# Eight pieces of a modulation product, moved out of three SSD groups: four into the value products, four ahead of the first group's projections

## The chip, the cores and the metric

The kernel runs on one core of a Trainium2 chip. The metric is device time in microseconds (us), the median of several runs of the same program. The engines in this text: PE is TensorE (matrix products), DVE is VectorE, ACT is ScalarE, POOL is GpSimd, SP is SyncE, which here issues DMAs. Each engine takes its instructions in order; semaphores tie the engines together.

## The reference

One layer of a diffusion backbone on 512 latent tokens of width 1024, with 256 context tokens. In float32:

```python
mod = silu(c) @ w_mod + b_mod                    # 6 x 1024 numbers
sh1, sc1, gt1, sh2, sc2, gt2 = split(mod, 6)
h   = rmsnorm(x, norm1_g) * (1 + sc1) + sh1      # and the same for ctx
p   = h @ w_in       # z, xBC, dt, q, k, v and two gates, in one product
ssd = bidirectional Mamba-2 scan (4 groups x 8 heads, chunks of 128 tokens)
att = windowed attention, 16 heads on 4 key/value heads, + all context keys
x   = x + gt1 * ((g_ssd * (ssd @ w_o_ssd) + g_att * (att @ w_o_att)) @ w_out)
x   = x + gt2 * conv_ffn(rmsnorm(x, norm2_g) * (1 + sc2) + sh2)
out = rmsnorm(x, final_g)
```

What the change touches is the first line. The columns of `sh1` and `sc1` are computed at the start; the other 4096 columns (`gt1, sh2, sc2, gt2`) are needed only behind both mixers, and the kernel spreads that work over the stages before.

## The kernel before, in words

A float32 product is made of three PE products: `split` writes a weight tile as a high part `whi` (ACT, a cast from `wraw`) and a low part `wlo` (DVE, a subtraction), and `gemm` issues high x high, high x low and low x high (L197, L198, L200). `load_raw` (L145) brings each weight tile of 512 KB from SP into a ring of three buffers `wraw`; `whi` and `wlo` have two each. `run` walks a list of steps, loads one step ahead and splits ahead of the product.

Stages by the trace: modulation and norm (to 57 us); first q and k products (57 to 76); the value products, `v_step` (76 to 96), 144 products of 320 columns into five `mis` banks and one `acc` bank of PSUM, followed by the copies into `vst` (ACT L699, DVE L700) and `te` (ACT L701); attention with projections beside it (96 to 367), for which the eight banks are cut anew into `acc`, `score`, `pt` and `po`, in an order that a planner sets; the SSD (367 to 722); merges, output products and FFN (to 1230).

The SSD starts with `proj_steps(0)`, the projections of the first of four groups of heads: a product, its convolution with SiLU (ACT `ta`, DVE `ta` L1268 and L1269, ACT `tb` L1275, DVE L1276 into `BT`, `tc` or `CT`), PE transposes of the result (L1295). Then for each group `ssd_steps(g)`: states, and for each chunk of 128 tokens `chunk_in` (loads tables into the buffers `fb` with four in the ring, and makes exponentials `E` from them on ACT and DVE, L1465 to L1471), `chunk_out` (PE products `mis<-st,CT` L1480 and `mis<-E,xs` L1486) and `chunk_sum` (DVE `z`, L1506); the next group's projections stand between these.

The modulation work is `m_step(i)`, 32 pieces of 512 KB: eight groups of 512 columns (`cg`), four pieces each (`kk`). A piece is two DVE operations, each multiplying a 128 x 512 block by `silu(c)` per row and adding it into `tm` (L581 the first of a column group, L583 the others). After the fourth piece of a column group, four PE transposes (L591) put `tm` into a `mis` bank, and DVE sums it (L593) and adds the bias (L594) into `mod2`. Its place in the list before:

```python
m = msteps[3 * g : 3 * g + 3] if g < 3 else []
```

so pieces 0 to 8 stand in groups 0, 1 and 2, three each, none in group 3; 9 to 31 stand in later stages. Outside the attention's planned part, a scheduler sets the order on SP, ACT and DVE from the program's order and dependencies.

Of the kernel before, what the change touches and what calls it, by code (L numbers as in the profile page):

```python
# [18 lines left out]
P = 128  # L19
D = 1024  # L20
L = 512
# [6 lines left out]
V_BMOD = 0  # L28
# [11 lines left out]
def raw(ap):  # L40
    return ap.bitcast(F32)
# [3 lines left out]
def tile_hybrid_layer(  # L45
# [32 lines left out]
    nc = tc.nc  # L78
    V, S, G, T = nc.vector, nc.scalar, nc.gpsimd, nc.tensor
# [17 lines left out]
    def bank(name):  # L97
        pool, w, tag = banks_[name]
        return pool.tile([P, 512 * w], F32, tag=tag, name=tag)
# [8 lines left out]
    def accb():  # L108
        return bank("acc")

    def misb():
        return bank("mis")
# [3 lines left out]
    def tmp(tag):  # L116
        return tpool.tile([P, 512], F32, tag=tag, name=tag, bufs=TMP[tag])
# [21 lines left out]
        src["up", i] = wup[i], 1024  # L139
    src["dn", 0] = wdn[0, 0], 1024  # L140

    def load_raw(key):
        a, n = src[key]
        r = wpool.tile([P, 1024], F32, tag="raw", name="wraw", bufs=3)
        nc.sync.dma_start(r[:, :n], a)  # L145
        return r, n

    def split(r, n, hi, lo):
        S.copy(hi[:, :n], r[:, :n])  # L149
        V.tensor_tensor(lo[:, :n], r[:, :n], raw(hi[:, :n]), ALU.subtract)  # L150

    def split_first(r, n, hi, lo):
        V.tensor_copy(hi[:, :n], r[:, :n])
# [51 lines left out]
    ident = cpool.tile([P, P], F32, name="ident")  # L205
    vec = cpool.tile([P, NV], F32, name="vec")
# [12 lines left out]
    mod2 = cpool.tile([P, 32], F32, name="mod2")  # L219
# [84 lines left out]
    with tc.tile_pool(name="spool", bufs=1) as sp:  # L304
# [131 lines left out]
        r, W, H = {}, {}, {}  # L436
# [50 lines left out]
        rows = {}  # L487
# [47 lines left out]
        for i in range(NG):  # L535
            t = tmp("tb")
# [33 lines left out]
    def m_step(i):  # L570
        cg, kk = i // 4, i % 4

        def fn(r):
            if kk == 0:
                macc[0] = tmp("tm")
            acc = macc[0]
            for u in range(2):
                k = 2 * kk + u
                sc = csil[:, k, 0:1]
                if k == 0:  # L580
                    V.tensor_scalar_mul(acc, r[:, 0:512], sc)  # L581
                else:
                    V.scalar_tensor_tensor(acc, r[:, u * 512 : u * 512 + 512], sc, acc, ALU.mult, ALU.add)  # L583
            if kk == 3 and cg > 5:
                ps = misb()
                T.matmul(ps, ones, acc, start=True, stop=True)
                V.tensor_tensor(F["g2"][cg - 6], ps, F["g2"][cg - 6], ALU.add)
            elif kk == 3:
                ps = misb()
                for c in range(4):  # L590
                    T.transpose(ps[:, c * P : (c + 1) * P], acc[:, c * P : (c + 1) * P], ident)  # L591
                z = slice(4 * cg, 4 * cg + 4)
                V.tensor_reduce(mod2[:, z], ps.rearrange("p (c q) -> p c q", c=4), axis=AX.X, op=ALU.add)  # L593
                V.tensor_tensor(mod2[:, z], mod2[:, z], vec[:, V_BMOD + 16 + 4 * cg : V_BMOD + 20 + 4 * cg], ALU.add)  # L594

        return [("m", i)], fn

# [4 lines left out]
    a2p = a2pool.enter_context(tc.tile_pool(name="a2pool", bufs=1, reuse_waits="tile"))  # L602
# [59 lines left out]

        return [("k", t)], fn

    Q, F = {}, {}

    def q_high(r, t):
        q = [attp.tile([P, L], F32R, tag="q", name="q", bufs=7) for _ in range(2)]
# [3 lines left out]
    def q_low(r, t):  # L672

        q = Q[2 * t], Q[2 * t + 1]
        lo = tmp("tc").bitcast(F32R)
        V.tensor_tensor(lo, r, raw(q[0]), ALU.subtract)
        for o, i in ((q[1][64:128, :], q[0][64:128, :]), (q[1][0:64, :], lo[64:128, :]), (q[0][64:128, :], lo[0:64, :])):
            nc.sync.dma_start(raw(o), raw(i))

    def q_split(ps, t):  # L680
        r = rope(ps, 1.0)
        q_high(r, t)
        q_low(r, t)

    def v_step(*w):

        pos = [misb() for _ in range(5)] + [accb()]
        for k in range(KT):
            wh, wl = (z[:, (k % 3) * 320 : (k % 3 + 1) * 320] for z in w[k // 3])
            for t, po in enumerate(pos):  # L690
                hh, hl, c0 = (hlh, hll, t) if t < 4 else (hch, hcl, t - 4)
                c, o = slice(c0 * P, (c0 + 1) * P), po[:, 0:320]
                T.matmul(o, hh[:, k, c], wh, start=k == 0, stop=False)
                T.matmul(o, hh[:, k, c], wl, start=False, stop=False)
                T.matmul(o, hl[:, k, c], wh, start=False, stop=k == KT - 1)
        steps = tmp("te")
        for t, po in enumerate(pos):
            o = po[:, 0:256].rearrange("p (h d) -> p h d", h=4)
            S.copy(vst[:, t, :, 0:64], o)  # L699
            V.tensor_tensor(vst[:, t, :, 64:128], o, raw(vst[:, t, :, 0:64]), ALU.subtract)  # L700
            S.copy(steps[:, t * 64 : (t + 1) * 64], po[:, 256:320])  # L701
        F["steps"] = steps
# [86 lines left out]
    def block_atoms(n, turned):  # L789
# [27 lines left out]
        def least(i):  # L817
            h = 4 * j + i
            p = d["p"][i] = a2p.tile([P, 640], F32, tag="p", name="p", bufs=NP_)
            V.tensor_tensor_reduce(  # L820
# [61 lines left out]
        for i in range(4):  # L882
# [5 lines left out]
            needs = ["S%d.%d" % (n, i)] + (["c%d" % (n - 2)] if n > 1 else [])  # L888
            if k >= NP_:
                f, g = of(k, NP_)  # L890
                needs.append("T%d.%d.%d" % (f, (3, 4, 4, 3)[f % 4], g))
# [323 lines left out]

        return some

    NP_ = 7
    BESIDE = [("q", 2), ("q", 3), ("z", 0), ("z", 1), ("k", 1), ("q", 4), ("z", 2), ("z", 3), ("q", 5), ("z", 4)]
    BESIDE += [("q", 6), ("z", 5), ("z", 6), ("q", 7)] + [("z", i) for i in range(7, 14)] + [("oa", 0), ("oa", 1)]  # L1220
    OLD = len(BESIDE)
# [40 lines left out]
    bp = bpool.enter_context(tc.tile_pool(name="bpool", bufs=1, reuse_waits="tile"))  # L1262
# [15 lines left out]
    def flat(a):  # L1278
        return a.rearrange("p a b -> p (a b)")
# [19 lines left out]
    def proj_steps(g):  # L1299
        d = GR[g]  # L1300

        def b_fn(w):
            d["xs"] = bp.tile([P, 4, 512], F32, tag="xs", name="xs", bufs=2)
            d["xsc"] = bp.tile([P, 2, 512], F32, tag="xsc", name="xsc", bufs=1)
            d["Bkc"] = bp.tile([P, 2, P], F32, tag="Bkc", name="Bkc", bufs=2)
            d["Bk"] = bp.tile([P, 4, P], F32, tag="Bk", name="Bk", bufs=2)
            d["BT"] = bp.tile([P, L], F32, tag="BT", name="BT", bufs=2)
            pl, pc = accb(), accb()
            gemm([LAT(pl)], w)
            turn()  # L1310
            gemm([CTX(pc)], w)
            conv_silu(pl, L, 16 + g, d["BT"])
            BTc = tmp("tc")
            conv_silu(pc, LC, 16 + g, BTc)
            for t, n, k in ((d["BT"], 4, d["Bk"]), (BTc, 2, d["Bkc"])):
                TURN.append((t, n, lambda ps, n=n, k=k: S.copy(flat(k), ps[:, : n * P])))

        def c_fn(w):
            d["CT"] = bp.tile([P, L], F32, tag="CT", name="CT", bufs=2)
            pl = accb()  # L1320
            gemm([LAT(pl)], w)
            turn()
            conv_silu(pl, L, 20 + g, d["CT"])

        def x_fn(ct, w):
            i = 4 * g + ct
            pl, pc = accb(), accb()
            gemm([LAT(pl)], w)
            turn()
            gemm([CTX(pc)], w)  # L1330
            for pp, n, dst in ((pl, L, d["xs"]), (pc, LC, d["xsc"])):
                xl = tmp("tc")
                conv_silu(pp, n, i, xl)
                TURN.append(
                    (
                        xl,
                        n // P,
                        lambda ps, n=n, dst=dst: S.copy(
                            dst[:, :, ct * P : (ct + 1) * P], ps[:, :n].rearrange("p (a b) -> p a b", b=P)
                        ),  # L1340
                    )
                )

        r = [([("x", 16 + g)], b_fn), ([("x", 20 + g)], c_fn)]
        for ct in range(4):
            r.append(([("x", 4 * g + ct)], lambda w, ct=ct: x_fn(ct, w)))
        return r
# [173 lines left out]
        return r + [([], gate)]  # L1521

    msteps = [m_step(i) for i in range(32)]
    prog = proj_steps(0)
    for g in range(4):
        s = ssd_steps(g)
        f = fill[n2 + g : n2 + 1 + g]
        b = proj_steps(g + 1) if g < 3 else fill[n2 + 4 : n3]
        m = msteps[3 * g : 3 * g + 3] if g < 3 else []

        prog += s[0:1] + f + b[0:1] + s[1:2] + m[0:1] + b[1:2]
        for c in range(4):
            prog += s[3 * c + 2 : 3 * c + 3] + (s[3 * c + 4 : 3 * c + 5] if c < 3 else [])
            if g == 3 and c:
                prog += s[3 * c : 3 * c + 1]
            prog += b[2 + c : 3 + c]
            if c == 1:
                prog += b[6:]
            if g < 3 or c == 3:
                prog += s[3 * c + 3 : 3 * c + 4]  # L1540
            if c in (1, 2):
                prog += m[c : c + 1]
        prog += s[13:14]
# [649 lines left out]
```

## Time and profile before

| what | us |
|---|---|
| median of 3 runs | 1231.55 (1231.36 to 1231.83) |
| the profiled execution | 1231.67 |
| its span | 1229.8 |
| PE busy | 1217.2 |
| DVE busy | 914.8 |
| ACT busy | 687.1 |

The span runs from the first to the last recorded instruction; 1.87 us of the profiled execution lie outside it. An engine's busy time is the time in which it executed something; the rest of the span it waited. The granted PE clock was 0.998 of full speed over the run. A row of the timeline reads: start in us, duration in us, engine, line, operation, output<-inputs, shape, count, and in brackets the idle time before it and what ended that. A grouped row reads: busy us, mean ns of one | idle us before. A row of DMA issues reads: queue, count, KB each, us from issue to landing. A row of waits: engine, what it waited to do, for whom: us in total, times, longest.

### The profile page before, as it was taken

The page shows a single profiled execution, that of the slowest core. Times are in us where ns is not written, and L with a number is a line of the kernel's source. Part 1 is how long each engine was busy: PE and PEld are TensorE (multiplying, and loading weights), DVE is VectorE, ACT ScalarE, POOL GpSimd, SP SyncE. Part 2 cuts the span into 40 slices and gives each one's busy share as a digit, 9 for nine tenths or more (in the row PEclk, how much of TensorE's full clock was granted, in tenths as well). Part 3 has the DMA queues.
Part 4 walks back from the last instruction along what each step waited for, and adds up shares of the span by engine and source line. Part 5 has one row for each costly group of instructions (what it writes and reads, how often), then busy time and mean ns, then how long its engine had stood idle before and what let it go on. Part 6 is the DMA issues. An engine that isn't in the chain of part 4 may idle for free.

```text
span 1229.8 us, 17483 instructions
## 1 busy us (share of the span) xinstructions
PE 1217.2 (99%) x6337; PEld 996.6 (81%) x6337; DVE 914.8 (74%) x1489; ACT 687.1 (56%) x1302; POOL 168.0 (14%) x174
## 2 busy tenths in 40 slices
PE   9999999999999999999999999999999999999997
PEld 6798888888878877777777778888988888888886
DVE  4757888888654698697886786677688788886557
ACT  4657788787443556566586572223544444545543
POOL 0000111121100033233352530000200000000000
PEclk9999999999999999999999999999999999999999
DMA  9653678777846235345346466677144444457785
GB/s 359 250 149 91 216 203 190 213 193 218 219 143 208 92 126 147 117 131 184 122 140 201 137 204 221 230 242 236 50 164 147 145 151 152 153 169 244 245 303 200
DMA packets 108630, 224.65 MB, mean 183 GB/s; under 512 B 9600, under 2 KB 48832, under 8 KB 108544
## 3 DMA queue, kind: packets, MB, share of 16 engines
q1 hardware_dynamic: 101056, 197.32, 49.0%
q0 software_dynamic: 6912, 25.17, 8.7%
q8 instruction: 50, 0.82, 0.3%
q10 hardware_dynamic: 576, 1.05, 0.2%
q14 instruction: 36, 0.29, 0.1%
HBM read 193.29 MB, written 49.87 MB: 198 GB/s over the span
## 4 chain that ended last, share of the span: by engine, by line
PE 92%; DVE 3%; DMA 2%; ACT 2%; issue 1%; SPq 0%; POOLq 0%; ACTq 0%; DVEq 0%
PE acc L197 19%; PE acc L200 19%; PE acc L198 19%; PE acc L1919 3%; PE acc L1917 3%; PE acc L1918 3%; PE score L811 3%; PE po L860 3%; PE pt L847 2%; PE mis L1480 2%; PE mis L1385 2%; DMA wm<-wm 1%; PE acc L930 1%; PE mis L422 1%; PE acc L931 1%; PE acc L932 1%
## 5 line engine op out<-in xcount | busy, mean ns | idle before, releaser
L197 PE MATMUL acc<-hlh,whi 128*128 128x512 f32 x488 | 199.3, 408 | 0.0
L150 DVE TENSOR_TENSOR wlo<-wraw,whi 128x1024 fp32r<-128x1024 f32 (+2 forms) x119 | 143.4, 1207 | 70.1 <-ACT whi L149 60.8
L200 PE MATMUL acc<-hlh,wlo 128*128 128x512 f32 x488 | 191.4, 392 | 0.0
L149 ACT CAST whi<-wraw 128x1024 fp32r<-128x1024 f32 (+2 forms) x119 | 122.6, 1033 | 122.4 <-PE acc L198 74.5
L198 PE MATMUL acc<-hll,whi 128*128 128x512 f32 x488 | 190.8, 391 | 0.0
L197 PE MATMUL acc<-mh,whi 128*128 128x512 f32 x360 | 141.0, 392 | 0.0
L200 PE MATMUL acc<-mh,wlo 128*128 128x512 f32 x360 | 140.1, 389 | 0.0
L198 PE MATMUL acc<-ml,whi 128*128 128x512 f32 x360 | 140.0, 389 | 0.0
L200 PEld LDWEIGHTS acc<-hlh,wlo 128*128 128x128 f32 x488 | 91.6, 188 | 20.4
L198 PEld LDWEIGHTS acc<-hll,whi 128*128 128x128 f32 x488 | 91.9, 188 | 17.5 <-issue 1.7
L197 PEld LDWEIGHTS acc<-hlh,whi 128*128 128x128 f32 x488 | 91.8, 188 | 17.6 <-issue 2.2
L198 PEld LDWEIGHTS acc<-ml,whi 128*128 128x128 f32 x360 | 67.6, 188 | 14.5 <-issue 0.5
L197 PEld LDWEIGHTS acc<-mh,whi 128*128 128x128 f32 x360 | 67.6, 188 | 14.4 <-issue 0.5
L200 PEld LDWEIGHTS acc<-mh,wlo 128*128 128x128 f32 x360 | 67.6, 188 | 14.0
L820 DVE CUSTOM_DVE_ANT_0 p<-score,winm,nsink 128x512 f32<-128x512 f32 (+1 forms) x64 | 51.8, 810 | 15.0 <-PE score L811 13.6
L1268 DVE SCALAR_TENSOR_TENSOR ta<-acc,half,ta 128x511 f32<-128x511 f32 (+1 forms) x66 | 43.8, 663 | 25.8 <-ACT ta L1267 25.8
L1267 ACT ACTIVATE ta<-acc,half 128x512 f32<-128x512 f32 (+1 forms) x66 | 46.8, 709 | 27.1 <-PE acc L200 25.9
L1275 ACT ACTIVATE tb<-ta 128x512 f32<-128x512 f32 (+1 forms) x44 | 23.5, 534 | 65.0 <-DVE ta L1269 59.0
L827 ACT ACTIVATE p<-p,mneg 128x512 f32<-128x512 f32 (+1 forms) x64 | 49.7, 777 | 15.3 <-DVE mneg L820 14.7
L1387 POOL TENSOR_TENSOR st<-st,eT 128x512 f32<-128x512 f32 x24 | 33.5, 1396 | 170.6 <-ACT st L1405 162.3
L197 PE MATMUL acc<-hch,whi 128*128 128x256 f32 x176 | 54.4, 309 | 0.0
L855 DVE TENSOR_TENSOR ptl<-pt,pth 128x512 fp32r<-128x512 f32 x72 | 47.5, 686 | 8.6 <-ACT pth L851 7.8
(512 smaller groups left out, 2972.7 us busy)
## 6 DMA issues: line engine op xcount, KB each, us to landing
wraw<-wup SPq DMA_DIRECT2D x44, 512.0 KB, 3.6
wt_d<-wdn POOLq DMA_DIRECT2D x36, 512.0 KB, 7.5
fb<-cs_d SPq DMA_DIRECT2D x32, 512.0 KB, 6.6
wraw<-wm SPq DMA_DIRECT2D x32, 512.0 KB, 4.3
wraw<-wx SPq DMA_DIRECT2D x24, 512.0 KB, 3.5
wraw<-wt_d SPq DMA_DIRECT2D x20, 512.0 KB, 4.3
sp_d<-te SPq DMA_DIRECT2D x33, 256.0 KB, 2.5
wm<-wm SPq DMA_DIRECT2D x16, 512.0 KB, 7.7
```

The source lines that it names most:

```text
L149: S.copy(hi[:, :n], r[:, :n])
L150: V.tensor_tensor(lo[:, :n], r[:, :n], raw(hi[:, :n]), ALU.subtract)
L197: T.matmul(ps, wh, xh[:, k0 + k, :], start=a, stop=False)
L198: T.matmul(ps, wh, xl[:, k0 + k, :], start=False, stop=False)
L200: T.matmul(ps, wl, xh[:, k0 + k, :], start=False, stop=b)
L811: T.matmul(ps[:, o : o + len(z) * P], Q[h][:, b * P : (b + 1) * P], k[:, j, z[0] * P : (z[-1] + 1) * P], start=v == 0 and o % 512 in (0, P ...
L820: V.tensor_tensor_reduce(p[:, :w], d["ps"][i][:, o0 : o0 + w], m, op0=ALU.add, op1=ALU.min, scale=1.0, scalar=nsink[:, h : h + 1], accum_o ...
L827: S.activation(p, p, AF.Exp, bias=d["mneg"][:, i : i + 1], scale=-1.0, accum_out=d["den"][:, i : i + 1])
L855: V.tensor_tensor(d["ptl"][x], d["pt"][x], raw(d["pth"][x]), ALU.subtract)
L860: T.matmul(d["po"], vst[:, cols[x], j, :], d[y][x], start=x == 0 and y == "pth", stop=x == c - 1 and y == "ptl")
L1267: S.activation(o[:, :n], ps[:, :n], AF.Identity, scale=hcol(base_w, stride + i), bias=hcol(base_b, i))
L1268: V.scalar_tensor_tensor(o[:, 1:n], ps[:, 0 : n - 1], hcol(base_w, i), o[:, 1:n], ALU.mult, ALU.add)
```

## The change

Pieces 0 to 3 (column group 0) are brought in `v_step` by eight DMAs of 128 x 512 into buffers that the attention will use later (`p`, six; `pth`, two). Their eight DVE operations are ordered behind the last `wlo` before the value products; the transposes and the sum follow the last value product and come ahead of the copies into `vst` in the program. Pieces 4 to 7 (column group 1) are brought by four DMAs into the ring `fb` before the first group's projections; their eight DVE operations stand there too, and their transposes and sum follow the third step of those projections. Piece 8 stays in group 0; groups 1 and 2 have none.

```diff
-            elif kk == 3:
-                ps = misb()
-                for c in range(4):
-                    T.transpose(ps[:, c * P : (c + 1) * P], acc[:, c * P : (c + 1) * P], ident)
...
+            elif kk == 3 and F.get("later"):
+                F["close"] = lambda: close(acc)
             elif kk == 3:
+                close(acc)
+        def close(acc):      # the lines taken out above: transposes, sum, bias
...
     def v_step(*w):
-        pos = [misb() for _ in range(5)] + [accb()]
+        pieces = []
+        for i in range(4):
+            if i < 3:
+                r = [a2p.tile([P, 640], F32, tag="p", name="p", bufs=NP_)[:, :L] for _ in range(2)]
+            else:
+                r = [raw(a2p.tile([P, L], F32R, tag="pth", name="pth", bufs=2)) for _ in range(2)]
+            for u in range(2):
+                nc.sync.dma_start(r[u], wm2[0, i, :, u * L : u * L + L])
+            pieces.append(r)
+        behind = F["low"].ins            # the last wlo
+        v_products(w)
+        with tc.issue_after(behind):
+            for i in range(4):
+                m_step(i)[1](pieces[i])
+        v_rows()
...
     msteps = [m_step(i) for i in range(32)]
+    mfirst = {0: msteps[8:9], 1: [], 2: [], 3: []}
+    pieces = []
+    for i in range(4):
+        f = bp.tile([P, 8, P], F32, tag="fb", name="fb", bufs=4)
+        nc.sync.dma_start(flat(f), wm2[1, i])
+        pieces.append(flat(f))
+    F["later"] = True
+    for i in range(4):
+        m_step(4 + i)[1](pieces[i])
+    F["later"] = False
     prog = proj_steps(0)
+    prog.insert(3, ([], lambda: F["close"]()))
...
-        m = msteps[3 * g : 3 * g + 3] if g < 3 else []
+        m = mfirst[g]
```

Line numbers grow by about 30 in the later parts. PE at the end of the value products, with what each instruction waits for (semaphores, by engine); first before, then changed:

```order
L694 MATMUL acc<-wlo,hch 128x320
L695 MATMUL acc<-whi,hcl 128x320
L811 MATMUL score<-khi,q 128x256 [waits DMAHW7_49,DMAHW4_49,Activation_49]
L811 MATMUL score<-klo,q 128x256 [waits DMAHW6_49]
L811 MATMUL score<-khi,q 128x256
L811 MATMUL score<-klo,q 128x256
L197 MATMUL acc<-hlh,whi 128x512
```

```order
L722 MATMUL acc<-wlo,hch 128x320
L723 MATMUL acc<-whi,hcl 128x320
L599 MATMUL mis<-ident,tm 128x128 [waits Activation_49]
L599 MATMUL mis<-ident,tm 128x128 x3
L841 MATMUL score<-khi,q 128x256 [waits DMAHW5_49,DMAHW1_49,DVE_49]
L841 MATMUL score<-klo,q 128x256 [waits DMAHW3_49]
L841 MATMUL score<-khi,q 128x256
L841 MATMUL score<-klo,q 128x256
L199 MATMUL acc<-hlh,whi 128x512
```

Four transposes of `tm` now stand between the last value product and the first score. The score waited for ACT's last copy out of the first value bank; now the transposes wait for that copy, and the score waits for DVE's sum out of the same bank. DVE at the same place, before and changed:

```order
L150 TENSOR_TENSOR wlo<-wraw,whi 128x640
L944 TENSOR_TENSOR wlo<-wraw,whi 128x1024
L700 TENSOR_TENSOR vst<-mis,vst 128x4x64 x5
L700 TENSOR_TENSOR vst<-acc,vst 128x4x64
L820 ISA p,mneg<-score,winm,nsink 128x512
```

```order
L152 TENSOR_TENSOR wlo<-wraw,whi 128x640
L584 TENSOR_SCALAR tm<-p,csil 128x512
L586 SCALAR_TENSOR_TENSOR tm<-p,csil,tm 128x512 x5
L586 SCALAR_TENSOR_TENSOR tm<-pth,csil,tm 128x512 x2
L974 TENSOR_TENSOR wlo<-wraw,whi 128x1024
L730 TENSOR_TENSOR vst<-mis,vst 128x4x64 x5
L730 TENSOR_TENSOR vst<-acc,vst 128x4x64
L601 TENSOR_REDUCE mod_89<-mis 128x4
L602 TENSOR_TENSOR mod_89<-mod_89,vec 128x4
L850 ISA p,mneg<-score,winm,nsink 128x512
```

The eight products stand between the two `wlo`; the sum stands behind all six subtractions into `vst`, ahead of the first softmax operation. DVE at the first group's projections, before and changed:

```order
L150 TENSOR_TENSOR wlo<-wraw,whi 128x1024 x2
L1268 SCALAR_TENSOR_TENSOR ta<-acc,half,ta 128x511
L1269 SCALAR_TENSOR_TENSOR ta<-acc,half,ta 128x511
L1276 SCALAR_TENSOR_TENSOR BT<-tb,ta 128x512
L1268 SCALAR_TENSOR_TENSOR ta<-acc,half,ta 128x255
L1269 SCALAR_TENSOR_TENSOR ta<-acc,half,ta 128x255
L150 TENSOR_TENSOR wlo<-wraw,whi 128x1024
L1276 SCALAR_TENSOR_TENSOR tc<-tb,ta 128x256
```

```order
L586 SCALAR_TENSOR_TENSOR tm<-fb,csil,tm 128x512 x2
L1297 SCALAR_TENSOR_TENSOR ta<-acc,half,ta 128x511
L586 SCALAR_TENSOR_TENSOR tm<-fb,csil,tm 128x512
L1298 SCALAR_TENSOR_TENSOR ta<-acc,half,ta 128x511
L586 SCALAR_TENSOR_TENSOR tm<-fb,csil,tm 128x512 x2
L1305 SCALAR_TENSOR_TENSOR BT<-tb,ta 128x512
L586 SCALAR_TENSOR_TENSOR tm<-fb,csil,tm 128x512
L1297 SCALAR_TENSOR_TENSOR ta<-acc,half,ta 128x255
L586 SCALAR_TENSOR_TENSOR tm<-fb,csil,tm 128x512
L1298 SCALAR_TENSOR_TENSOR ta<-acc,half,ta 128x255
L152 TENSOR_TENSOR wlo<-wraw,whi 128x1024
L1305 SCALAR_TENSOR_TENSOR tc<-tb,ta 128x256
```

Seven of the eight products now stand between the operations of one convolution (the first stands ahead of the rows shown), all ahead of the `wlo` and the `tc` that PE takes next. PE's transposes of that `tc` moved behind one matmul of the next product. SP at that place, before and changed:

```order
L145 DMA wraw<-wx 128x1024
L972 DMA ao_d<-te 128x512
L145 DMA wraw<-wx 128x1024
L1433 DMA z<-zs_d 128x512 x2
L972 DMA ao_d<-te 128x512
L145 DMA wraw<-wx 128x1024
L1433 DMA z<-zs_d 128x512 x2
L1445 DMA fb<-cs_d 128x8x128 x4
```

```order
L147 DMA wraw<-wx 128x1024
L1002 DMA ao_d<-te 128x512
L147 DMA wraw<-wx 128x1024
L1557 DMA fb<-wm 128x1024
L1002 DMA ao_d<-te 128x512
L1557 DMA fb<-wm 128x1024 x3
L147 DMA wraw<-wx 128x1024
L1462 DMA z<-zs_d 128x512 x4
L1474 DMA fb<-cs_d 128x8x128 x2
```

One load of a piece stands ahead of the store `ao_d<-te`, three behind it and ahead of the third `wraw<-wx`; the loads `z` and the first tables `fb<-cs_d` come after. In group 1, two `tm` stood in DVE's row between `xw` and the first `E` (L1469); that place is now:

```order
L1305 SCALAR_TENSOR_TENSOR CT<-tb,ta 128x512
L1485 SCALAR_TENSOR_TENSOR coef<-TT,cbd,bcs 128x8
L1402 TENSOR_TENSOR xw<-xs,TD 128x512
L1498 COPY_PREDICATED E<-sel,eb 128x512
L1500 TENSOR_TENSOR E<-E,mis 128x512
```

The first `E` follows `xw` directly.

More of the change, by code (lines that the diff above doesn't have):

```diff
@@ L140, in tile_hybrid_layer @@
     src["dn", 0] = wdn[0, 0], 1024
+    F = {}
     def load_raw(key):
@@ L149, in split @@
         S.copy(hi[:, :n], r[:, :n])
-        V.tensor_tensor(lo[:, :n], r[:, :n], raw(hi[:, :n]), ALU.subtract)
+        F["low"] = V.tensor_tensor(lo[:, :n], r[:, :n], raw(hi[:, :n]), ALU.subtract)
     def split_first(r, n, hi, lo):
@@ L576, in fn @@
             acc = macc[0]
+            rows = r if isinstance(r, list) else [r[:, u * 512 : u * 512 + 512] for u in range(2)]
             for u in range(2):
@@ L580, in fn @@
                 if k == 0:
-                    V.tensor_scalar_mul(acc, r[:, 0:512], sc)
+                    V.tensor_scalar_mul(acc, rows[0], sc)
                 else:
-                    V.scalar_tensor_tensor(acc, r[:, u * 512 : u * 512 + 512], sc, acc, ALU.mult, ALU.add)
+                    V.scalar_tensor_tensor(acc, rows[u], sc, acc, ALU.mult, ALU.add)
             if kk == 3 and cg > 5:
@@ L587, in fn @@
                 V.tensor_tensor(F["g2"][cg - 6], ps, F["g2"][cg - 6], ALU.add)
+            elif kk == 3 and F.get("later"):
+                F["close"] = lambda: close(acc)
             elif kk == 3:
-                ps = misb()
-                for c in range(4):
-                    T.transpose(ps[:, c * P : (c + 1) * P], acc[:, c * P : (c + 1) * P], ident)
-                z = slice(4 * cg, 4 * cg + 4)
-                V.tensor_reduce(mod2[:, z], ps.rearrange("p (c q) -> p c q", c=4), axis=AX.X, op=ALU.add)
-                V.tensor_tensor(mod2[:, z], mod2[:, z], vec[:, V_BMOD + 16 + 4 * cg : V_BMOD + 20 + 4 * cg], ALU.add)
+                close(acc)
+        def close(acc):
+            ps = misb()
+            for c in range(4):
+                T.transpose(ps[:, c * P : (c + 1) * P], acc[:, c * P : (c + 1) * P], ident)
+            z = slice(4 * cg, 4 * cg + 4)
+            V.tensor_reduce(mod2[:, z], ps.rearrange("p (c q) -> p c q", c=4), axis=AX.X, op=ALU.add)
+            V.tensor_tensor(mod2[:, z], mod2[:, z], vec[:, V_BMOD + 16 + 4 * cg : V_BMOD + 20 + 4 * cg], ALU.add)
         return [("m", i)], fn
@@ L663, in k_step @@
         return [("k", t)], fn
-    Q, F = {}, {}
+    Q = {}
     def q_high(r, t):
@@ L683, in q_split, with v_products @@
         q_low(r, t)
+    NP_ = 7
     def v_step(*w):
-        pos = [misb() for _ in range(5)] + [accb()]
+        pieces = []
[13 more added lines that the diff above has]
+        v_rows()
+    def v_products(w):
+        pos = F["pos"] = [misb() for _ in range(5)] + [accb()]
         for k in range(KT):
@@ L695, in v_step, with v_rows @@
                 T.matmul(o, hl[:, k, c], wh, start=False, stop=k == KT - 1)
+    def v_rows():
         steps = tmp("te")
-        for t, po in enumerate(pos):
+        for t, po in enumerate(F.pop("pos")):
             o = po[:, 0:256].rearrange("p (h d) -> p h d", h=4)
@@ L1216, in weight_sums @@
         return some
-    NP_ = 7
     BESIDE = [("q", 2), ("q", 3), ("z", 0), ("z", 1), ("k", 1), ("q", 4), ("z", 2), ("z", 3), ("q", 5), ("z", 4)]
```

## The prediction

> **What bounds the kernel now.** I read the page's busy shares first, then its chain that ended last, then TensorE's waits in the SSD stage (300 to 730 us), where most of the moved work stands today.
>
> ```profile
> PE 1217.2 (99%) x6337; PEld 996.6 (81%) x6337; DVE 914.8 (74%) x1489; ACT 687.1 (56%) x1302; POOL 168.0 (14%) x174
> PE 92%; DVE 3%; DMA 2%; ACT 2%; issue 1%; SPq 0%; POOLq 0%; ACTq 0%; DVEq 0%
> ```
>
> TensorE (PE) is busy 99% of the span and carries 92% of the chain; VectorE (DVE), which this change relieves in one place and loads in another, carries 3%. So only what makes PE wait counts. The four head groups, one per stretch, then the modulation products (`tm`) on DVE in the same stretches:
>
> ```profile
> 420.00:500.00 80.00, 79.75 (x444) 61.30 (x443) 67.07 (x104) 48.17 (x114) 24.44 (x18) 1.00 0.41 128
> 500.00:580.00 80.00, 79.02 (x441) 60.60 (x440) 65.41 (x103) 50.03 (x117) 29.93 (x21) 1.00 0.47 143
> 580.00:660.00 80.00, 79.48 (x446) 61.64 (x445) 65.43 (x104) 50.60 (x118) 31.52 (x22) 1.00 0.47 145
> 660.00:722.00 62.00, 62.00 (x297) 44.23 (x296) 43.10 (x67) 40.48 (x98) 28.42 (x21) 1.00 0.49 154
> 420.00:500.00 80.00, 6.99 (x6) 1.00 0.41 128
> ...
> 660.00:722.00 62.00, 0.00 (x0) 1.00 0.49 154
> PE mis L1486 <- DVE E L1471: 0.9, 1, 0.9
> PE mis L1385 <- DVE z L1506: 0.5, 1, 0.5
> ```
>
> In the first rows the columns after the stretch's length are PE, PE's weight loads, DVE, ACT, POOL; the short rows are DVE's `tm` time alone, for the first and the last stretch. The three groups with pieces leave PE idle 0.25 + 0.98 + 0.52 = 1.75 us; the fourth, without pieces, leaves 0.00. The waits name 1.4 us of it, a row at 485 us below the rest. That is the whole prize in these groups, however much DVE work leaves them.
>
> **Part 1, what leaves the groups.** Eight pieces go, one (piece 8) stays: 16 DVE products, and with each closed column group four PE transposes, a reduction and an addition.
>
> ```profile
> L583 DVE SCALAR_TENSOR_TENSOR tm<-wraw,csil,tm 128x512 f32<-128x512 f32 x15 | 15.8, 1056 | 1.4 <-DMA wraw<-wm 1.2
> L581 DVE TENSOR_SCALAR tm<-wraw,csil 128x512 f32<-128x512 f32 x3 | 1.4, 478 | 1.6 <-DMA wraw<-wm 1.6
> L593 DVE TENSOR_REDUCE mod<-mis 128x4 f32<-128x512 f32 x2 | 1.4, 675 | 0.0
> 539.23 0.66 PE L1486 MATMUL mis<-E,xs 128*64 128x128 f32 x8
> 540.78 0.66 PE L1486 MATMUL mis<-E,xs 128*64 128x128 f32 x8 [0.90 <-DVE E L1471]
> 533.41 2.33 DVE L583 SCALAR_TENSOR_TENSOR tm<-wraw,csil,tm 128x512 f32<-128x512 f32 x2
> 540.04 0.69 DVE L1471 TENSOR_TENSOR E<-E,mis 128x512 f32<-128x512 f32 x1
> 633.96 1.09 PE L1486 MATMUL mis<-E,xs 128*64 128x128 f32 x16
> 635.57 1.12 PE L1385 MATMUL mis<-xw,Bk 128*128 128x512 f32 x2 [0.52 <-DVE z L1506]
> 633.42 1.10 DVE L1276 SCALAR_TENSOR_TENSOR tc<-tb,ta 128x512 f32<-128x512 f32 x1 [0.76 <-ACT tb L1275]
> 479.41 1.67 DVE L583 SCALAR_TENSOR_TENSOR tm<-wraw,csil,tm 128x512 f32<-128x512 f32 x1 [0.59 <-DMA wraw<-wm]
> 485.27 1.13 PE L1480 MATMUL mis<-st,CT 128*128 128x512 f32 x2 [0.25 <-ACT xs L1338]
> ```
>
> About 14 x 1.056 + 2 x 0.478 = 15.7 us of DVE time leave, off PE's path but for three places. At 540 us, 2.33 us of `tm` stand in DVE's queue ahead of the chain of exponents (`E`) that PE waits for. By starts, that wait is worth more than its 0.90: eight `mis<-E,xs` took 540.78 - 539.23 = 1.55, while sixteen took 1.09 at 633.96, so eight are near 0.5 and 1.05 is lost. All of it goes, since E ends 0.9 after PE wants it and 2.3 is taken out ahead. At 485 us a `tm` of 1.67 that itself waited 0.59 for its weights stands ahead of the exponents that ACT waits for before its copy `xs`; start to start I put 0.4 on it, and it goes. At 635.6 no `tm` product stands ahead in DVE's queue: `tc` there waited for ACT, and the reduction comes after `z`. I leave that 0.5 where it is. Next to be late is ACT: it already releases `tc`, with 0.76. **Gain 1.5 us; ends 0 (another wait follows each) and 2.1 (all three by starts, the one on `z` being 635.57 - 633.96 less about 1.0).** The eight PE transposes and the reductions only move; weight loads on SP also only move.
>
> **Part 2, four pieces in the value products (76 to 96 us).** Eight DMAs of 256 KB and eight DVE products enter; the transposes follow the last value product, and the scores take over the bank that they fill.
>
> ```profile
> 91.87 1.23 DVE L944 TENSOR_TENSOR wlo<-wraw,whi 128x1024 fp32r<-128x1024 f32 x1 [7.46 <-ACT whi L941]
> 94.23 2.18 DVE L700 TENSOR_TENSOR vst<-mis,vst 128x256 fp32r<-128x256 f32 x5 [1.13 <-ACT vst L699]
> 96.43 0.42 DVE L700 TENSOR_TENSOR vst<-acc,vst 128x256 fp32r<-128x256 f32 x1
> 96.77 0.74 DVE L820 CUSTOM_DVE_ANT_0 p<-score,winm,nsink 128x512 f32<-128x512 f32 x1
> 95.83 0.28 PE L811 MATMUL score<-khi,q 128*128 128x256 f32 x1
> 84.31 0.58 SPq L145 DMA_DIRECT2D wraw<-wq  x1
> wraw<-wq SPq DMA_DIRECT2D x2, 512.0 KB, 4.1
> 90.00:94.00 4.00, 4.00 (x29) 4.00 (x29) 1.23 (x1) 1.23 (x2) 0.00 (x0) 1.00 0.00 0
> ```
>
> The products cost nothing: 0.48 + 7 x 0.75 = 5.7 us fit in DVE's idle 7.46 ahead of 91.87, from 84.4 on. The last two of the eight DMAs are issued on SP where `wraw<-wq` goes out now, 84.3; with its 4.1 us they land by about 88.6 and DVE is free by 90.2, ahead of that `wlo`. SP's two `wq` loads behind them move some 1.2 us back, and the bus is empty (0.00) from 90 to 94 to take that up. The close does cost. PE used to start the first score at 95.83. Now the transposes run first (four at 0.11 from start to start, 0.44, no addition, since they leave the groups), to 96.27; the first score then waits for the reduction, which stands behind `vst<-acc` on DVE and so begins where `p<-score` began, 96.77, and takes 0.68 by its own row: 97.45, and 0.05 to PE. PE's queue behind that score holds the first of the projections, so nothing fills the gap. **Loss 97.5 - 96.3 = 1.2 us; ends 0.8 and 1.5**, by DVE and ACT reaching `vst<-acc` up to 0.4 earlier or 0.3 later.
>
> **Part 3, four pieces before the first group (364 to 382 us).** Four loads of 512 KB go out on SP around the store `ao_d<-te`, ahead of the third `wraw<-wx`, and the eight products interleave with the convolution on DVE.
>
> ```profile
> 373.79 0.75 DVE L1268 SCALAR_TENSOR_TENSOR ta<-acc,half,ta 128x511 f32<-128x511 f32 x1 [4.22 <-ACT ta L1267]
> 378.73 0.42 DVE L1276 SCALAR_TENSOR_TENSOR tc<-tb,ta 128x256 f32<-128x256 f32 x1
> 381.56 0.38 PE L1295 MATMUL mis<-ident,tc 128*128 128x128 f32 x2
> 382.24 0.40 PE L200 MATMUL acc<-hlh,wlo 128*128 128x512 f32 x1
> 368.82 0.32 SPq L972 DMA_DIRECT2D ao_d<-te  x1
> wraw<-wx SPq DMA_DIRECT2D x3, 512.0 KB, 4.4
> fb<-cs_d SPq DMA_DIRECT2D x2, 512.0 KB, 8.0
> ```
>
> The first piece can leave before 368 us and its two products fall into DVE's idle 4.22. The other three leave after that store, from about 369.2; at 4.0 to 4.4 us the second lands near 373.2, and the rest while DVE is at work. From there DVE holds six `tm` (4.0 us at the 0.67 from one start to the next), two long `ta` (1.6), BT (0.6), two short `ta` (0.9), `wlo` (1.1) and `tc` (0.4): 8.7, to 381.9. `tc` ended at 379.15 before, so the slack is nearly eaten: PE transposed `tc` at 381.56, but one matmul has been put ahead of it, so it is wanted at about 381.8, and `wlo`, done near 381.5, at 382.2. **Loss 0.15 us; ends 0 and 1.0**, for a second piece 0.2 early or 0.9 late. The deferred close adds only its transposes, 0.44, which left the groups. The four loads of `fb<-cs_d` wait for buffers that the products free, and land some 40 us before the stage that reads them.
>
> [...] If all three landed with the last, at about 375.6, the sum would be 1233.7, with the second piece 2.4 late; that is the milder form of rival A.
>
> **Sum.** The profiled execution took 1231.67 us (span 1229.8), 0.12 above the median of 1231.55. 1231.67 - 1.5 + 1.2 + 0.15 = **1231.5 us**. A measurement of this kernel tells 0.2%, 2.5 us, from no change, hardly less.
>
> **Rivals.** *A, slower: the pieces land late before the first group.* DVE works in order, so a `tm` that waits for its weights holds `ta`, `wlo` and `tc` behind it, and PE stops at 381.8. The price is the lateness less the slack. At 8.0 us, as `fb<-cs_d` had, the second piece lands at 377.2, 4.0 late; PE then stands 4.0, and the time is 1231.5 - 0.15 + 4.0 = 1235.3. It decides (over 1234.0) from 2.7 late. For it: four loads leave almost together. Against: 4.4 us was the median for `wraw<-wx` on the same queue in these 13 us. *B, no gain in the groups:* ACT, which already releases DVE there, takes the place of each wait: 1231.5 + 1.5 = 1233.0. For it: the waits at 485 and at 635 both run through ACT. Against: at 540 the chain has 2.3 us of `tm` directly ahead. *C, the close doesn't hold the scores:* DVE gets through the reduction before PE asks, and Part 2 is free: 1231.5 - 1.2 = 1230.3, with all 2.1 gained 1229.7. Against: the reduction is ordered behind `vst<-acc`. *D, DVE bounds the groups after all:* the 15.7 us come off in full, 1231.5 + 1.5 - 15.7 = 1217.3; against it stands the 1.75 us idle of PE.
>
> ```profile
> 1000.00:1100.00 100.00, 100.00 (x441) 82.45 (x440) 83.03 (x125) 47.62 (x70) 0.00 (x0) 1.00 0.47 153
> 646.33 1.88 PE L1480 MATMUL mis<-st,CT 128*128 128x512 f32 x4
> ```
>
> D has one more reading. The first four windows hold 227.77 us of weight loads in 302, 75.4%, where pure products hold 82.45%; that looks like 26 us of hidden waiting. But undisturbed SSD products start 1.88 / 4 = 0.47 apart at most, against 100 / 441 = 0.23, with one load each either way, so slower products explain the low share. [...]
>
> **How the numbers follow.** Forecast 0.52; A beyond 1234.0, 0.11; B and the milder A up to 1234.0, 0.21; C 0.11; D, or part of it below 1229.0, 0.05. The range leaves out A's 0.11, D's 0.05 and little else: from C with all the gain, 1229.7, to B with Part 3 at its end, 1233.85, and 0.2 more on either side for the scatter of the runs (1231.36 to 1231.83): 1229.5 to 1234.0. Faster by over 0.2%: D, 0.05, and a tail of C, 0.01. Slower: A, 0.11. Within: 0.83.
>
> **What would show it.** Right: in the changed profile the first score starts near 97.5 with about 1.2 us idle, released by DVE's reduction; the `tm` on `p` and `pth` lie between 84 and 91; `tc` ends near 381.9 and PE is idle by 0.2 or less there; the wait of PE on `E` in group 1 is gone and the one on `z` stays. Wrong: a wait of PE on DVE between 375 and 390 of over 1 us; a second large wait in the attention stage, where everything starts 1.65 later; or new waits on ACT in groups 0 to 2.

## The result, and the profile after

The changed kernel takes 1229.54 us (19 runs, 1228.99 to 1230.80) where the kernel before took 1231.75 in the same series: ratio 0.9982, 95% interval 0.9975 to 0.9989. In a later series it was 1229.45, ratio 0.9979 (0.9970 to 0.9988). So 2.2 us are gained; the forecast was 1231.5 us, next to no gain on the 1231.55 known then. The profiled execution took 1229.21 us, its span is 1227.4.

The page's busy shares and chain, then PE's whole list of waits, of the changed kernel:

```profile
PE 1216.9 (99%) x6337; PEld 997.3 (81%) x6337; DVE 912.9 (74%) x1489; ACT 686.4 (56%) x1302; POOL 166.1 (14%) x174
PE 96%; DMA 2%; DVE 1%; ACT 0%; issue 0%; SPq 0%; POOLq 0%; DVEq 0%; ACTq 0%
PE acc L457 <- POOL still L350: 1.1, 1, 1.1
PE score L841 <- DVE mod L601: 1.1, 1, 1.1
PE acc L243 <- DVE nsink L487: 0.3, 1, 0.3
PE acc L376 <- DMA wm<-wm: 0.2, 1, 0.2
```

DVE's busy time is nearly the same, 912.9 us after 914.8: the work has moved. Its share of the chain fell from 3% to 1%. All three waits of the SSD groups are gone, and one new wait stands at the first score. The groups' stretches (columns as in the prediction):

```profile
420.00:500.00 80.00, 80.00 (x450) 62.21 (x449) 63.66 (x99) 48.78 (x116) 23.66 (x18) 1.00 0.34 104
500.00:580.00 80.00, 80.00 (x447) 62.19 (x446) 61.98 (x98) 50.93 (x119) 29.30 (x21) 1.00 0.43 133
580.00:660.00 80.00, 80.00 (x447) 62.21 (x446) 61.49 (x97) 51.26 (x121) 31.01 (x22) 1.00 0.45 136
660.00:722.00 62.00, 62.00 (x294) 44.22 (x294) 43.66 (x66) 41.02 (x97) 30.15 (x22) 1.00 0.49 153
```

PE has no idle time left there, and in the first three stretches 450, 447 and 447 matmul records stand where there were 444, 441 and 446. The end of the value products, PE and then DVE:

```profile
95.39 0.31 PE L723 MATMUL acc<-whi,hcl 128*128 128x320 f32 x1
95.54 0.60 PE L599 MATMUL mis<-ident,tm 128*128 128x128 f32 x4
97.22 0.39 PE L841 MATMUL score<-khi,q 128*128 128x256 f32 x1 [1.08 <-DVE mod L601]
96.14 0.42 DVE L730 TENSOR_TENSOR vst<-acc,vst 128x256 fp32r<-128x256 f32 x1
96.48 0.68 DVE L601 TENSOR_REDUCE mod<-mis 128x4 f32<-128x512 f32 x1
```

PE stops for the sum, which stands behind the last subtraction into `vst`. The first group's projections, DVE and then PE:

```profile
374.26 0.75 DVE L586 SCALAR_TENSOR_TENSOR tm<-fb,csil,tm 128x512 f32<-128x512 f32 x1 [2.27 <-DMA fb<-wm]
381.35 1.22 DVE L152 TENSOR_TENSOR wlo<-wraw,whi 128x1024 fp32r<-128x1024 f32 x1
382.49 0.41 DVE L1305 SCALAR_TENSOR_TENSOR tc<-tb,ta 128x256 f32<-128x256 f32 x1
383.01 0.39 PE L1324 MATMUL mis<-ident,tc 128*128 128x128 f32 x2
383.47 0.39 PE L202 MATMUL acc<-hlh,wlo 128*128 128x512 f32 x1
```

DVE starts on the second piece as it lands, at 374.26; everything there stands 1.2 us later than before, and `tc` and `wlo` are done just ahead of PE.

To see where the 2.4 us of the two spans went, I matched PE's instructions of the two traces in their order and took the difference of their starts (after less before; each step is a change of that difference):

| place (time in before) | difference behind it | step | what it is |
|---|---|---|---|
| start, to 57 | -0.24 | -0.24 | the first weights: PE waited 1.4 for them, now 0.2 |
| first score, 95.83 | +1.39 | +1.63 | transposes 0.44, wait 1.19 |
| attention, to 355 | +1.22 | -0.17 | +0.11 right behind the first score, whose successor starts 0.22 after it and not 0.11; -0.28 at a wait on `de` that is gone |
| projections, 382 | +1.14 | -0.08 | nothing |
| 390 | +1.60 | +0.46 | transposes of column group 1 |
| 485 to 487 | +0.84 | -0.76 | group 0: ACT `xs`, then `E` |
| 518 | +0.34 | -0.50 | transposes that left |
| 540 to 570 | -1.42 | -1.76 | group 1: 1.10 on `E`, 0.66 in three smaller steps |
| 632 | -1.86 | -0.44 | transposes that left |
| 635 to 637 | -2.57 | -0.71 | group 2: the wait on `z` |
| the end, 1222 | -2.43 | +0.14 | nothing of the change |

The transposes cancel (+0.90, -0.94). What is left is +1.30 at the scores (1.19 and 0.11) and -3.23 in the groups.

### The profile page after: what moved, and what is told of

Its sections match the earlier page's. It is cut to its first block, busy times and chain, and to the rows that moved or that the text cites. A ratio compares the mean times of both kernels' runs of the same rounds, so it can differ in the third digit from the quotient of the medians.

```text
span 1227.4 us, 17505 instructions
## 1 busy us (share of the span) xinstructions
PE 1216.9 (99%) x6337; PEld 997.3 (81%) x6337; DVE 912.9 (74%) x1489; ACT 686.4 (56%) x1302; POOL 166.1 (14%) x174
## 3 DMA queue, kind: packets, MB, share of 16 engines
q10 hardware_dynamic: 576, 1.05, 0.2%
## 4 chain that ended last, share of the span: by engine, by line
PE 96%; DMA 2%; DVE 1%; ACT 0%; issue 0%; SPq 0%; POOLq 0%; DVEq 0%; ACTq 0%
PE acc L199 20%; PE acc L202 20%; PE acc L200 20%; PE acc L1957 3%; PE acc L1959 3%; PE acc L1958 3%; PE score L841 3%; PE po L890 3%; PE pt L877 2%; PE mis L1509 2%; PE mis L1414 2%; PE mis L1515 1%; DMA wm<-wm 1%; PE acc L960 1%; PE acc L962 1%; PE acc L961 1%
```

## The experiments

Each was timed against the kernel before in the same series (1231.79 to 1231.88 us there).

**The halves.** Pieces 0 to 3 in the value products, the others in the groups:

```diff
-    mfirst = {0: msteps[8:9], 1: [], 2: [], 3: []}
+    mfirst = {0: [], 1: [nop] + msteps[4:6], 2: msteps[6:9], 3: []}
     # nop is a step that does nothing; no pieces are taken ahead of proj_steps(0)
```

> The changed kernel with only its first half: pieces 0 to 3 in the value products; pieces 4 and 5 stay in group 1, 6 to 8 in group 2, group 0 has none. Theory (the gain sits where pieces leave a group, and the close costs the scores 1.2 us): +1.2 at the scores, -0.8 for group 0, between 0 and -1.3 in group 1, nothing in group 2, so 1231.0 to 1232.2 against 1231.75 for before. Rival (the gain is a lucky order of the attention or of the scheduler, not the pieces): near the changed kernel, 1229.5, or near before plus 1.2, 1233, wherever the pieces stand.

It took 1234.57 us, ratio 1.0019 (1.0010 to 1.0027): slower than before by 2.7, outside what I expected. Its trace agrees with the theory up to 1100 us, where it stands 1.0 ahead of the kernel before (+1.67 at the scores, -0.74 in group 0, -1.40 at 540 in group 1). Then comes a wait in the FFN that neither the kernel before nor the changed kernel has. PE's longest wait and its row:

```profile
PE acc L1948 <- DVE tc L1842: 2.5, 1, 2.5
1115.04 0.47 PE L1948 MATMUL acc<-ww,fyh 128*128 128x512 f32 x1 [2.53 <-DVE tc L1842]
```

This is the first product of the down part. For it the eight banks are cut anew into `acc`, and its first bank is bank 0. In this kernel the last up product, which DVE still reads at L1842, had come to stand in bank 0 of PSUM too; in the kernel before it stands in bank 1, in the changed kernel in 2. Its place in the ring of five `mis` banks follows from how the banks went round since the ring was made, and a close taken out ahead moves it.

The other half, pieces 4 to 7 ahead of the projections and 0 to 3 left in groups 0 and 1, 8 in group 2:

```diff
-    mfirst = {0: msteps[8:9], 1: [], 2: [], 3: []}
+    mfirst = {0: msteps[0:3], 1: msteps[3:4], 2: [nop, nop, msteps[8]], 3: []}
     # and v_step without pieces
```

> The changed kernel with only its second half: pieces 4 to 7 ahead of the first group's projections; 0 to 2 stay in group 0, 3 in group 1, 8 at the end of group 2. Theory: no wait at the scores, 0 to +0.2 in the projections, group 0 as before, group 1 and group 2 gain 1.3 to 2.4: 1229.4 to 1230.6. Rival (order by luck): no gain, 1231.7.

It took 1231.22 us, ratio 0.9994 (0.9985 to 1.0003): no gain that is clear of the scatter. As expected, there is no wait at the scores and none in the projections (the step there is -0.04), group 1 gains 1.7, and in group 2 the wait on `z` is gone (-0.72). But 1.7 is lost again in group 2, by starts, in two waits on `E` (1.12 and 0.62; the list of waits shows 1.3 of it). The larger comes behind these rows of DVE; what makes the smaller, at 648, was not traced:

```profile
611.69 1.28 DVE L584 TENSOR_SCALAR tm<-wraw,csil 128x512 f32<-128x512 f32 x1
613.01 1.67 DVE L586 SCALAR_TENSOR_TENSOR tm<-wraw,csil,tm 128x512 f32<-128x512 f32 x1
619.37 0.69 DVE L1487 TENSOR_TENSOR E<-E,mis 128x512 f32<-128x512 f32 x1
PE mis L1502 <- DVE E L1487: 1.3, 2, 0.9
```

Piece 8 has moved: before, its two products ran at 643.6, since `tm` has one buffer and column group 1 held it until its transposes at 631.7. With that group closed long before, they run as soon as their weights are there, ahead of `E`, and take 2.95 us where the pair at 643.6 took 1.22.

**The bank.** Values only, with one more bank taken from the ring at the end of the SSD (a write of one column), and the changed kernel with the same line:

```diff
     run(prog)
+    for _ in range(1):
+        V.memset(misb()[:, 0:1], 0.0)
     bpool.close()
```

> Values only again, with one bank of the mis ring taken (a write of one column, 128 x 1) and never used at the end of the SSD, so that the last product of the FFN's up part stands in bank 3 and not in bank 0, which the first down product takes over. Theory: the 2.5 us wait of PE on DVE at 1113 us was that shared bank; it goes, and 1231.87 + 1.2 - 2.2 = 1230.9 is left. Rival (the wait is the pieces' late DVE work): 1234.5 as before.

> The changed kernel with one bank of the mis ring taken in the same way, which puts its last up product into bank 0 (2 without this). Theory: the same wait of 2.5 us appears at the first down product, and nothing else changes: 1229.54 + 2.7 = 1232.2, so the changed kernel's gain would be lost to a bank number 700 us later. Rival: the wait belonged to the other kernel alone, 1229.5.

The line puts the last up product into bank 3 in the first and into bank 0 in the second. The first took 1230.94 us, ratio 0.9992 (0.9983 to 1.0001): the wait is gone, and the theory's number holds. The second took 1233.11 us, ratio 1.0010 (1.0001 to 1.0018): the wait has come, and with it the changed kernel is slower than the kernel before. It came out 0.9 above what I expected; the last section shows where that comes from. The rows show the wait, a PE row further on, and the granted clock (the column after POOL) in 1112 to 1120 us:

```profile
1113.39 0.47 PE L1959 MATMUL acc<-ww,fyh 128*128 128x512 f32 x1 [2.53 <-DVE tc L1853]
1115.41 0.63 PE L1960 MATMUL acc<-ww,fyl 128*128 128x512 f32 x1
1112.00:1120.00 8.00, 6.61 (x22) 5.31 (x23) 7.96 (x13) 4.98 (x8) 0.00 (x0) 0.79 0.83 286
```

Up to that point the two changed kernels' traces differ by 0.2 us at most. So the bank explains the wait in both directions. Without it the median of "values only" lies 0.9 us below the kernel before, in an interval that still holds no difference.

**The close.** The transposes of pieces 0 to 3 go into a free `acc` bank, ahead of the last eighth of the value products; the products are ordered ahead of `v_products` in the program, still behind the last `wlo`:

```diff
...                                     # close takes the bank as an argument
-        behind = F["low"].ins
-        v_products(w)
-        with tc.issue_after(behind):
+        F["later"] = True
+        with tc.issue_after(F["low"].ins):
+            for i in range(4):
+                m_step(i)[1](pieces[i])
+        F["later"] = False
         v_products(w)
...
         for k in range(KT):
+            if k == KT - 1:
+                F["close"](accb())
```

> The changed kernel with the close of pieces 0 to 3 moved: the four transposes go into a free acc bank ahead of the last eighth of the value products, and the sum stands ahead of the subtractions into vst. Theory: the products are done 2.9 us before the transposes, the first score finds its bank without DVE's sum, the wait of 1.1 goes: 1229.54 - 1.2 = 1228.3. Rival: the scores then wait for something else that ends as late (ACT's copies, or vst set back by the sum's 0.8 us), and the time stays within 0.4 of 1229.5.

It took 1228.40 us, ratio 0.9971 (0.9961 to 0.9981). PE's rows and DVE's sum, from the profile of the repeat below:

```profile
93.21 0.60 PE L599 MATMUL acc<-ident,tm 128*128 128x128 f32 x4
96.14 0.31 PE L726 MATMUL acc<-whi,hcl 128*128 128x320 f32 x1
96.29 0.28 PE L844 MATMUL score<-khi,q 128*128 128x256 f32 x1
93.84 0.69 DVE L601 TENSOR_REDUCE mod<-acc 128x4 f32<-128x512 f32 x1 [0.63 <-PE acc L599]
```

The first score follows the last value product at once. The sum falls into time in which DVE was idle: its first `vst` starts at 94.69, 1.45 us ahead of PE's last value product, as in the changed kernel (93.94 against 95.39). Since 1.1 us is little beside the scatter of the runs, both ran again in one series:

> The changed kernel itself, beside the early close on one chip: 1229.5.

> The early close again, beside the changed kernel. Theory: 1.2 below it, 1228.3. Rival (the difference was between chips): within 0.4 of it.

They took 1229.45 us (ratio 0.9979, 0.9970 to 0.9988) and 1228.40 (0.9971, 0.9960 to 0.9982). That is 1.05 us apart, where the first runs, in two series, lay 1.14 apart. Between these two traces the start of the first score steps by -1.59, of which 0.4 are the transposes that now stand earlier. This is the fastest of the kernels that do all the work. The intervals of the two ratios overlap; that it is faster rests on the repeat, on the medians and on the wait that is gone.

**What the pieces cost in the groups.** Without pieces 0 to 7; and with their loads alone:

```diff
-        m = msteps[3 * g : 3 * g + 3] if g < 3 else []
+        m = msteps[8:9] if g == 0 else []                       # no pieces
...
+    V.memset(mod2, 0.0)                                         # in both
+    msteps[:8] = [(k, lambda r: None) for k, _ in msteps[:8]]   # loads only
```

> The kernel before without pieces 0 to 7, which are left out altogether (their columns of mod2 are set to zero); piece 8 stays in group 0. Theory: everything the eight pieces cost before goes: waits of 3.2 us and eight transposes, 0.9: 1231.75 - 4.1 = 1227.6. So the changed kernel pays 1.2 for the close, 0.9 for transposes and nothing for the sixteen DVE products. Rival (DVE work hides more than waits show): under 1226.

> The kernel before with pieces 0 to 7 loaded in their places into wraw, but their sixteen DVE products, the transposes and the sums left out (their columns of mod2 are zero). Theory (the DVE products were what held PE): as without the pieces, 1227.4 to 1227.8. Rival (the weight loads in the ring of three, or the DMA traffic, held the next weights): most of the 3.2 us of waits stay, 1230 to 1231.

Without pieces it took 1227.44 us, ratio 0.9965 (0.9952 to 0.9977), the theory's number. PE stands 4.4 ahead at the end, by the same steps in the groups as in the changed kernel, which lies 2.1 above it: the close and eight transposes. With the loads only it took 1229.43 us, ratio 0.9980 (0.9971 to 0.9989), below the rival's range and far above the theory's. Groups 0 and 1 gain in full (-0.74 and -1.76 without the transposes), and 1.8 is lost again at 618 and 634. The first of these two places:

```profile
609.35 1.28 DVE L581 TENSOR_SCALAR tm<-wraw,csil 128x512 f32<-128x512 f32 x1
610.67 1.67 DVE L583 SCALAR_TENSOR_TENSOR tm<-wraw,csil,tm 128x512 f32<-128x512 f32 x1
618.12 0.66 PE L1486 MATMUL mis<-E,xs 128*64 128x128 f32 x8 [0.90 <-DVE E L1471]
```

It is piece 8 again, which this kernel left in group 2. With piece 8 taken in group 0:

```diff
-        m = msteps[3 * g : 3 * g + 3] if g < 3 else []
+        m = msteps[3 * g : min(3 * g + 3, 8)] if g < 3 else []
...
-        prog += s[0:1] + f + b[0:1] + s[1:2] + m[0:1] + b[1:2]
+        prog += s[0:1] + f + b[0:1] + s[1:2] + m[0:1] + (msteps[8:9] if g == 0 else []) + b[1:2]
```

> Loads only, as the last one of that kind, but with piece 8 taken in group 0 instead of group 2, where its two DVE products had moved up to 609 us and ahead of E. Theory (loads cost PE nothing; the 2.0 us between the two kernels were piece 8's place): as the kernel without pieces, 1227.4 to 1227.8, no wait of PE at 617 and 632. Rival (the loads of pieces 6 and 7 hold something in group 2): 1229.0 to 1229.5 again.

It took 1227.83 us, ratio 0.9968 (0.9956 to 0.9979): as without pieces, by the same steps of PE, and with no wait in group 2. So the loads cost PE nothing that these runs show; the DVE work of the pieces did, products and sums together. And this one piece in a bad place costs 1.8 us by starts (1.6 by the two medians), about half of the 3.2 that the eight others cost before.

**The slack of the projections.** Two more products there:

```diff
         m_step(4 + i)[1](pieces[i])
+    for u in range(2):
+        V.scalar_tensor_tensor(macc[0], pieces[3][:, u * L : u * L + L], csil[:, u, 0:1], macc[0], ALU.mult, ALU.add)
```

> The changed kernel with two more products of the same form in the first group's projections (the last piece added in twice more, which changes column group 1 of mod2), 1.3 us of DVE ahead of wlo and tc. Theory (the slack of that place is eaten to about 0.2 us): PE stops there for 1.0 to 1.3 us, and the time is 1230.5 to 1230.8. Rival (slack is left): 1229.5 to 1229.8, no wait of PE between 375 and 390.

It took 1229.75 us, ratio 0.9983 (0.9974 to 0.9992): the rival's number, though PE does lose 0.74 at that place. The order had changed with it: `tc` went ahead of the last product, and PE had two products on context rows and the deferred transposes to put into the gap,

```profile
383.94 0.28 PE L200 MATMUL acc<-hcl,whi 128*128 128x256 f32 x1
384.06 0.60 PE L599 MATMUL mis<-ident,tm 128*128 128x128 f32 x4
384.66 0.50 PE L202 MATMUL acc<-hlh,wlo 128*128 128x512 f32 x1
```

so a part of the work that stood later in the changed kernel (the transposes at 391.36) was done while it waited. This run therefore doesn't measure the slack itself. How late the loads may come (rival A) wasn't tried.

## Why the prediction was right or wrong

The time lies 0.04 us inside the lower edge of the range, 1229.5, and in the later series, at 1229.45, 0.05 outside it. That it lies inside is luck: I had set that edge for a close that costs nothing and all of the gain that I held possible (rival C), but the close cost what I forecast, and the groups gave more. The sum was 2.0 us too high, 1.7 of it in one term. By its steps:

*The close at the scores* (1.2): it cost 1.19 up to the first score, released by DVE's sum, and 1.30 up to the second; the kernel without this wait is 1.05 to 1.14 faster by the medians. Right in mechanism and size.

*The projections* (0.15): they cost nothing (the step is -0.08). The second piece was there 1.06 later than the 373.2 forecast, on a stage that stood 1.2 later, and `tc` ended at 382.90, against 381.9 + 1.2. Right; rival A didn't come. The 8.0 us of `fb<-cs_d` that I set against it were no case of four loads leaving together: SP issued those four from 370.99 to 378.17, behind loads of `z`. Here three pieces were issued from 370.43 to 371.81, and they took 3.7, 4.9 and 5.8 us, so they came one behind the other and not all with the last.

*The products in the value stage* (nothing): right; they ran from 84.04 to 90.04 in one row.

*The gain in the groups* (1.5, ends 0 and 2.1): this is the step that failed. It measured 3.23, beyond its upper end; the kernels without the eight pieces' DVE work confirm it. The parts: 485 us, 0.76 for my 0.4; 540 us, 1.76 for my 1.05; 635 us, 0.71 for my 0. Two errors are in it. First, I took each listed wait and the one place it stood at. PE's first start behind `E` gained 1.10, near the 1.05 that I worked out, but three smaller steps behind it (0.30, 0.23, 0.13) are in no list of waits, because PE is drawn as busy there. The second of them, in the kernel before, stands in four products that undisturbed take 1.88:

```profile
565.80 2.11 PE L1480 MATMUL mis<-st,CT 128*128 128x512 f32 x4
```

The 0.23 are inside the 2.11. So the idle 1.75 us, which I called the whole prize, were no upper bound. Second, I kept the wait on `z` because no `tm` stood directly ahead of it and ACT released the row before. But DVE works through a backlog there. In the changed kernel all the work there stands earlier, and one operation stands behind `z` and not ahead; DVE before, then changed:

```profile
634.45 0.47 DVE L1268 SCALAR_TENSOR_TENSOR ta<-acc,half,ta 128x255 f32<-128x255 f32 x1
634.84 0.67 DVE L1506 TENSOR_TENSOR z<-mis,z 128x512 f32<-128x512 f32 x1
630.92 1.26 DVE L1305 SCALAR_TENSOR_TENSOR tc<-tb,ta 128x512 f32<-128x512 f32 x1 [0.76 <-ACT tb L1304]
632.11 0.68 DVE L1535 TENSOR_TENSOR z<-mis,z 128x512 f32<-128x512 f32 x1
633.84 0.47 DVE L1297 SCALAR_TENSOR_TENSOR ta<-acc,half,ta 128x255 f32<-128x255 f32 x1
```

Against before, `z` is 2.73 earlier and PE there 2.44. Most of it is the backlog: `tc`, ahead of `z`, already starts 2.50 earlier (633.42 before); it still waits 0.76 for ACT, but that wait moved along with the rest. Likewise at 540: in "values only" both products of the 2.33 us row still stand directly ahead of `E`, yet the wait is gone. What had left DVE's queue there are two other products and the sum and addition of column group 0; before, then "values only":

```profile
522.94 0.68 DVE L593 TENSOR_REDUCE mod<-mis 128x4 f32<-128x512 f32 x1
525.34 0.47 DVE L581 TENSOR_SCALAR tm<-wraw,csil 128x512 f32<-128x512 f32 x1
525.86 0.75 DVE L583 SCALAR_TENSOR_TENSOR tm<-wraw,csil,tm 128x512 f32<-128x512 f32 x1
532.35 2.33 DVE L586 SCALAR_TENSOR_TENSOR tm<-wraw,csil,tm 128x512 f32<-128x512 f32 x2
```

From 520 to that row DVE gains 1.86 on the kernel before, 0.8 behind it at first and 1.06 ahead at the end (532.35 for 533.41). The row that I named was not the cause by itself.

*Rivals.* B (ACT takes the place of each wait) didn't come: no wait of PE is left there. C didn't come in this kernel; the early close shows what it is worth. D didn't come: 15.7 us of DVE left the groups and PE got 3.2 back; without the eight pieces at all it gets 4.4, with their transposes. The low share of weight loads, which looked like 26 us of hidden waiting, is 230.84 of 302 us now, 76.4% after 75.4%, with every wait gone: slower products, as the sum had it.

What stays open: the 0.24 at the start and the 0.28 at the wait on `de` in attention, 0.5 together. The first differs between the profiles of all these kernels (-0.31 to +0.29 against before, at 57 us). The second stands in every profile of a kernel with pieces in the value products (eight) and in none without (four, where the wait on `de` stays); what links it to them I didn't test.

## What to carry to other kernels

Where an in-order engine feeds the bottleneck just in time, size the relief by the backlog that leads up to a late operation, not by the row ahead of it (here 3.23 us came for the 1.5 read off the rows ahead), and compare starts of the bottleneck's instructions rather than its idle time. A small work unit that closes a product should find a bank and a place in the queue ahead of the evacuations that the next stage waits for (here 1.1 us). After any change that alters how often a ring of banks is used, look at the next place where the banks are cut anew: there a shift of one or two banks was worth more (2.6 us and over) than the whole change.

## What the runs showed that I had not expected

Behind the same wait of 2.53 us the granted clock was 1.00 in the profile of "values only" (1.00 in 1112 to 1120 us) and lower in that of the changed kernel with bank 0. There the clock stands at 0.50 in 1114.7 to 1118.0 us and at 1.00 on both sides (0.71 over 1113 to 1117 us, 0.86 over 1117 to 1121, 0.79 over the 8 us above). From 1114.98 to 1117.97 the matmuls start 0.43 apart instead of 0.23, and by the two shares, 4 x 0.29 + 4 x 0.14, an estimated 1.7 us are lost on top of the wait. What decided between the two outcomes, no run here shows.

Both outcomes come in the same kernel. Of the eleven runs of each of the two, six had a mean granted clock of 0.996 or 0.997 and five of 0.998; without the wait it was one run of eleven ("values only" with the next bank) and one of nineteen (the changed kernel). The six took longer: a median of 1233.56 us against 1232.17 with bank 0, and 1234.80 against 1233.59 in "values only". The 1232.17 is the 1232.2 that I had expected, so the 0.9 that I missed goes with the clock; where it fell is recorded for the profiled run alone.

DVE's two operations of one piece took 0.46 to 0.49 and 0.73 to 0.76 us wherever no operation of POOL ran beside them, in all thirteen profiles. Beside POOL the second took 1.27 to 1.88 (19 times, six of them in the kernel before), and the first 1.28 in the two kernels where piece 8 stands at 609 to 614 us (twice it took no longer than alone, with POOL beside it for 0.35 us). POOL's rows at that time, in the loads-only kernel:

```profile
608.76 1.59 POOL L1387 TENSOR_TENSOR st<-st,eT 128x512 f32<-128x512 f32 x1
610.31 1.47 POOL L1366 TENSOR_TENSOR ssq<-ssq,sq 128x512 f32<-128x512 f32 x1
```

In the changed kernel POOL is at 0.00 in both stretches that took pieces (84 to 90 and 371 to 381 us), and none of the sixteen products there took over 0.75. So the move also shortened these products, from 17.3 us of busy time for eighteen to 1.24 for the two that stayed and 11.5 for the sixteen others. DVE's busy time over the whole span fell by 1.9 us only, and no run changed POOL's work alone.
